# Feed-forward input of a 2048-frame encoder layer: gate and up products by turns instead of block by block

## The chip, the cores and the metric

The kernel runs on one core of a Trainium2 chip. The metric is the device time of one execution in microseconds (us). Engines are named as in the profile: PE (TensorE, the matmuls), PEld (TensorE's weight loads, beside PE), DVE (VectorE), ACT (ScalarE), POOL (GpSimd) and SP (SyncE, which issues all the large transfers of this stage in one queue).

## The reference, cut to what matters

```python
for l in range(DEPTH):                                   # DEPTH = 1, x: 2048 x 1024, fp32
    h = rmsnorm(x, mix_norm_g[l])
    proj = jnp.einsum('bsd,de->bse', h, w_in[l])
    q, k, v, u, vg = jnp.split(proj, split_pts, axis=-1)
    a = band_attention(q, k, v, q_norm_g[l], k_norm_g[l], rel_bias[l])
    g = spatial_gating(u, vg, sgu_norm_g[l], w_spatial[l], b_spatial[l])
    mix = jnp.concatenate([rmsnorm(a, att_out_norm_g[l]), rmsnorm(g, gmlp_out_norm_g[l])], axis=-1)
    x = x + jnp.einsum('bse,ed->bsd', mix, w_out[l])
    h = rmsnorm(x, ffn_norm_g[l])
    gate, up = jnp.split(jnp.einsum('bsd,df->bsf', h, w_ffn_in[l]), 2, axis=-1)
    x = x + jnp.einsum('bsf,fd->bsd', jax.nn.silu(gate) * up, w_ffn_out[l])
```

The change lies in the line with `gate, up` (1024 to 2 x 2816 columns) and in `silu(gate) * up`.

## The kernel before, in words

Every fp32 operand is split in two parts that PE takes at its faster rate: `split` (lines 86 to 88) writes the rounded value h with a cast on ACT (line 87) and the rest l with a subtraction on DVE (line 88); `mm3` (lines 90 to 93) makes a product of three matmuls: h by h (L91), h by l (L92), l by h (L93). So `wih` and `wil` are the two parts of a weight operand, and `yh` and `yl` those of an activation operand.

The stages follow each other: input projection, attention, output projection, feed-forward input (lines 701 to 797), feed-forward output. Both feed-forward matrices go by Winograd's scheme of seven products for a 2 x 2 block product.

**Activation operands.** For each of 16 row tiles, `operands(m)` transposes the normalized tile `h2` on PE (`pth`, L606), copies it to `hT` (ACT, L607), makes four sums t1 to t4 on POOL (L618 to L621) and writes seven operand pieces to memory in `y_d` (SP, L623). `prep(hf)` later loads the seven operands of one half of the rows (`ynat`, four transfers each, into the three buffers of the pool `gt`, which also hold the result tile `g`) and splits them into yh0..yh6 and yl0..yl6. There is one buffer for each of the seven, so those of the second half can be written only when the first half's last product with the same number is done.

**Weight operands.** `weights(p, s)` loads two raw tiles `wir` (512 KB each), makes four sums s1 to s4 on POOL (L733 to L736) and splits seven operands. s is 0 for gate and 1 for up, p is one of 11 pairs of column blocks. The operands stand in a ring of eight `wih` and eight `wil`.

**Products.** `block(w, ys, g, s)` runs the seven products of one side one after another, each of 4 x 3 matmuls of 128x512 into a PSUM bank. ACT copies v1 and v, DVE makes u2 and the sums `g` (gate) or `up`, ACT applies silu, POOL multiplies (L757). Two halves, 11 pairs, two sides, seven products and 12 matmuls are 3696 matmuls. After each pair, POOL and DVE make three sums `c` (L791 to L794), and SP writes `g` and `c` to `f_d` (L796, L797).

**Feed-forward output.** For each of 11 rounds the next stage loads an activation operand `ar` from `f_d` and a weight (`w11_0`, `w11_2`, ... in the first 11 rounds, in buffers of their own; later ones in `wor`), and splits them into ah, al, oh, ol.

**What sets the order.** The tile framework's scheduler sets each engine's order from the program's dependences and from when pool memory comes free; on PE the attention stage's order is written out by hand. A new pool takes the memory of closed ones, and its first writer then waits for their last reader. SP's transfers run through eight completion semaphores in turn, so an issue also waits until the transfer eight before it has landed.

Of the kernel before, what the change touches and what calls it, by code (L numbers as in the profile page):

```python
# [18 lines left out]
P = 128  # L19
# [12 lines left out]
NF = DFF // P  # L32
# [11 lines left out]
def block_kernel(ctx: ExitStack, tc: tile.TileContext, x, xT, w_in, mixg, qg, kg, bias, sgug, wsT, bsp, outg, w_out, ffng, w_fi, w_fo, out):  # L44
    nc = tc.nc
# [30 lines left out]
    def pool(stack, name, bufs, side="left", space=bass.MemoryType.SB):  # L76
        return stack.enter_context(tc.tile_pool(name=name, bufs=bufs, side=side if space != PSUM else None, space=space, reuse_waits="tile"))
# [8 lines left out]
    def split(hi, lo, src):  # L86
        nc.scalar.copy(hi, src)  # L87
        nc.vector.tensor_sub(lo, src, hi.bitcast(F32))  # L88

    def mm3(ps, lh, ll, rh, rl, first, last):  # L90
        nc.tensor.matmul(ps, lhsT=lh, rhs=rh, start=first, stop=False)  # L91
        nc.tensor.matmul(ps, lhsT=lh, rhs=rl, start=False, stop=False)  # L92
        nc.tensor.matmul(ps, lhsT=ll, rhs=rh, start=False, stop=last)  # L93
# [4 lines left out]
    apool = {}  # L98
    bt, vt, qd, kw, pvs, sums, xm, gn, an, mh, ml, heads = ({} for _ in range(12))

    def open_attention(stack):
        for n, bufs in (("pr", 3), ("pp", 2), ("an", 2), ("sa", 4), ("vt", 6), ("bt", 1), ("qd", 2), ("kw", 5)):
            apool[n] = pool(stack, n, bufs, "right")


    woh, wol, mx = {}, {}, {}
# [138 lines left out]
    with ExitStack() as st:  # L245
# [240 lines left out]
        w = [None] * 4  # L486
# [20 lines left out]
        wr = raw.tile([P, G, P], F32, tag="raw", name="wsr")  # L507
# [12 lines left out]
        for hf in range(2):  # L520
            for b, unit in enumerate(blocks):
                for tl in range(8):
                    t = hf * 8 + tl
# [26 lines left out]
                w = nw  # L550


    with ExitStack() as st:
        st_att = st.enter_context(ExitStack())
        open_attention(st_att)
        st_wr.close()
        hp = pool(st_out, "h2", 1)
# [85 lines left out]
        def feed(k, whole):  # L643
            while fill:
                kind, f = fill[0]
                if kind in ("piece", "bank"):
                    if k < 1 or kind == "bank" and not whole:
                        break
                    f()
                    k -= 1  # L650
                elif kind == "operands":
                    operands(f)
                elif kind == "g":
                    load_xm(f)
# [13 lines left out]
        with tc.manual_schedule(engines={mybir.EngineType.PE}):  # L668
            for m in range(NE):
                an[m] = None  # L670
            for _ in range(3):
                k = feed(KT, True)
            for i in range(len(LATE) + 2):
                if i < len(LATE):
                    m, h = LATE[i]
# [7 lines left out]
                k = feed(k + 1, False)  # L683
                if 1 <= i <= len(LATE):
                    flip(*LATE[i - 1], sp)
                k = feed(k + 1, True)
                if i >= 2:
                    m, h = LATE[i - 2]
# [10 lines left out]


    with ExitStack() as st:
        gt, wr, sp3, wi = (pool(st, n, b, "right") for n, b in (("gt3", 3), ("wr3", 2), ("sum3", 1), ("wi3", 8)))
        yp = [pool(st, f"y{i}", 1) for i in range(2)]
        tm = pool(st, "tm3", 2)
        yp += [pool(st, f"y{i}", 1, "left" if i < 5 else "right") for i in range(2, 7)]
        cb = pool(st, "cb3", 1, "right")
        pb = [pool(st, f"pb{i}", 4, space=PSUM) for i in range(2)]

        def bank(s):
            return pb[s].tile([P, 512], F32, tag="b", name="bank")  # L710

        def prep(hf):
            ys = []
            for o in range(7):
                yh = yp[o].tile([P, 4, 512], F32R, tag="yh", name=f"yh{hf}{o}")
                yl = yp[o].tile([P, 4, 512], F32R, tag="yl", name=f"yl{hf}{o}")
                ys.append((yh, yl))
                r = gt.tile([P, 4, 512], F32, tag="g", name="ynat")
                for i in range(4):
                    nc.sync.dma_start(r[:, :, i * P : (i + 1) * P], y_d[hf][o][i].rearrange("p (k t) -> p k t", k=4))  # L720
                for k in range(0, 4, 2):
                    split(yh[:, k : k + 2], yl[:, k : k + 2], r[:, k : k + 2])
            return ys

        def weights(p, s):
            r = []
            for i in range(2):
                t = wr.tile([P, 2, 512], F32, tag="wr", name="wir")
                nc.sync.dma_start(t, w_fi[2 * p + i, s])
                r.append(t)  # L730
            x11, x12, x21, x22 = r[0][:, 0], r[0][:, 1], r[1][:, 0], r[1][:, 1]
            s1, s2, s3, s4 = (sp3.tile([P, 512], F32, tag=f"s{i}", name=f"s{i}") for i in range(4))
            nc.gpsimd.tensor_add(s1, x21, x22)  # L733
            nc.gpsimd.tensor_sub(s2, s1, x11)  # L734
            nc.gpsimd.tensor_sub(s3, x11, x21)
            nc.gpsimd.tensor_sub(s4, x12, s2)  # L736
            ops = []
            for src in (x11, s2, s1, s3, x12, s4, x22):
                h = wi.tile([P, 4, P], F32R, tag="wih", name="wih")
                l = wi.tile([P, 4, P], F32R, tag="wil", name="wil")  # L740
                split(h, l, src.rearrange("p (k f) -> p k f", k=4))
                ops.append((h, l))
            return ops

        def product(bk, w, y):
            for k in range(4):
                mm3(bk, w[0][:, k], w[1][:, k], y[0][:, k], y[1][:, k], k == 0, k == 3)

        def block(w, ys, g, s):
            def emit(i, bk, add):  # L750
                if s == 0:
                    nc.vector.tensor_tensor(g[:, i], bk, add, op=ALU.add)
                    nc.scalar.activation(g[:, i], g[:, i], AF.Silu)
                else:
                    t = tm.tile([P, 512], F32, tag="up", name="up", bufs=1)
                    nc.vector.tensor_tensor(t, bk, add, op=ALU.add)  # L756
                    nc.gpsimd.tensor_tensor(g[:, i], t, g[:, i], op=ALU.mult)  # L757

            ba, bb, bc, bd = (bank(s) for _ in range(4))
            v1 = tm.tile([P, 512], F32, tag="v1", name="v1")  # L760
            u2 = tm.tile([P, 512], F32, tag="u2", name="u2")
            v = tm.tile([P, 512], F32, tag="v", name="v", bufs=1)
            product(ba, w[0], ys[0])
            nc.scalar.copy(v1, ba)
            product(bb, w[1], ys[1])
            nc.vector.tensor_tensor(u2, bb, v1, op=ALU.add)
            product(bc, w[2], ys[2])
            nc.scalar.copy(v, bc)
            nc.gpsimd.tensor_tensor(v, v, u2, op=ALU.add)
            product(bd, w[3], ys[3])  # L770
            nc.vector.tensor_tensor(u2, bd, u2, op=ALU.add)
            emit(3, bd, v)
            product(ba, w[4], ys[4])
            emit(0, ba, v1)
            product(bc, w[5], ys[5])
            emit(1, bc, v)
            product(bd, w[6], ys[6])
            emit(2, bd, u2)

        w = weights(0, 0)  # L780
        for hf in range(2):
            ys = prep(hf)
            for p in range(NF // 2):
                g = gt.tile([P, 4, 512], F32, tag="g", name="g")
                for s in range(2):
                    block(w, ys, g, s)
                    nx = 2 * p + s + 1
                    if nx < NF or hf == 0:
                        w = weights(*divmod(nx % NF, 2))
                c = cb.tile([P, 3, 512], F32, name="c", tag="c")  # L790
                nc.gpsimd.tensor_add(c[:, 0], g[:, 1], g[:, 3])  # L791
                nc.gpsimd.tensor_sub(c[:, 1], c[:, 0], g[:, 0])
                nc.gpsimd.tensor_sub(g[:, 1], g[:, 0], g[:, 1])
                nc.vector.tensor_sub(c[:, 2], g[:, 2], c[:, 1])  # L794
                hs = slice(hf * 512, (hf + 1) * 512)
                nc.sync.dma_start(f_d[p][0:4, :, hs].rearrange("o p t -> p o t"), g)  # L796
                nc.sync.dma_start(f_d[p][4:7, :, hs].rearrange("o p t -> p o t"), c)  # L797


    with ExitStack() as st:  # L800
        xo, t4, wk0, wt, ca, cb = (
            pool(st, n, b, "right") for n, b in (("xo4", 8), ("tm4", 4), ("wk40", 1), ("wt4", 3), ("ca4", 1), ("cb4", 1)))
        at, ar, wk, wr = (pool(st, n, b) for n, b in (("at4", 2), ("ar4", 3), ("wk4", 1), ("wr4", 4)))
        pb = [pool(st, f"pb4{i}", 4, space=PSUM) for i in range(2)]
# [118 lines left out]
```

## Time and profile before

| | us |
|---|---|
| median of 3 runs | 2212.45 (2211.03 to 2214.38) |
| the profiled execution, its own time | 2214.4 |
| span of that execution | 2212.6 |
| feed-forward input on PE | 919.4 to 1785.6 of the span |
| PE busy | 2162.9, 98% of the span |

PE is busy 98% of the span, so a gain can come only from stretches in which PE waits or runs at a lower clock. The profile's rows give start and duration in us of the span. In a timeline row "x2" joins neighbours of one kind, and the bracket at its end is the idle time of that engine just before it and what ended it. In a table by windows each engine has its busy time and, in brackets, the number of instructions; PEclk is the granted share of TensorE's full clock. Matmuls are pipelined: a duration of 0.39 us goes with a start every 0.226 us.

### The profile page before, as it was taken

How to read it: one execution, taken by the hardware profiler on the slowest of the kernel's cores; microseconds unless marked ns; L12 is line 12 of the kernel's file. 1: busy time of each engine (PE TensorE's matmuls, PEld its weight loads, DVE VectorE, ACT ScalarE, POOL GpSimd, SP SyncE). 2: the span in 40 equal slices, each digit the busy share in tenths (PEclk: the TensorE clock that was granted, in tenths of full speed). 3: DMA queues.
4: the chain of work that ended last, by engine and by line, in shares of the span. 5: the costliest groups of instructions: out<-in, count | busy, mean ns of one | idle time of the engine just before them, and what ended most of it. 6: DMA issues, size and time to landing. Idle time of an engine off the chain costs nothing.

```text
span 2212.6 us, 31917 instructions
## 1 busy us (share of the span) xinstructions
PE 2162.9 (98%) x12090; PEld 1796.8 (81%) x12090; DVE 1275.4 (58%) x1809; ACT 899.7 (41%) x1639; POOL 912.4 (41%) x792
## 2 busy tenths in 40 slices
PE   8999999999999999799999998999999999999999
PEld 7888887887888888688888886888888888888787
DVE  3467435774667666685555558556555534545555
ACT  6444534552565665443333335333232323222322
POOL 1264113330002200756666575575656512603444
PEclk9999999999999999999999999999999999999999
DMA  7243615648878874832323236232322363833463
GB/s 253 86 124 119 233 58 162 172 135 260 284 229 275 264 241 145 291 132 91 116 90 116 96 128 194 92 123 91 114 100 94 111 238 133 290 122 119 157 234 135
DMA packets 183802, 356.60 MB, mean 161 GB/s; under 512 B 15328, under 2 KB 68576, under 8 KB 182112
## 3 DMA queue, kind: packets, MB, share of 16 engines
q1 hardware_dynamic: 183504, 354.55, 48.5%
q8 instruction: 95, 1.56, 0.3%
q14 instruction: 59, 0.48, 0.1%
q10 hardware_dynamic: 144, 0.00, 0.0%
HBM read 253.83 MB, written 100.66 MB: 160 GB/s over the span
## 4 chain that ended last, share of the span: by engine, by line
PE 71%; issue 11%; POOL 6%; DVE 6%; DMA 3%; ACT 1%; SPq 1%; DVEq 0%; POOLq 0%; ACTq 0%
PE bank L91 16%; PE bank L93 16%; PE bank L92 16%; PE ps L91 5%; PE ps L92 5%; PE ps L93 5%; DVE wil L88 1%; PE S L177 1%; PE pt L204 1%; PE po L91 1%; PE po L93 1%; PE po L92 1%; POOL g L757 1%; PE pv L216 1%; POOL rhr L83 1%
## 5 line engine op out<-in xcount | busy, mean ns | idle before, releaser
L92 PE MATMUL bank<-yl,wih 128*128 128x512 f32 x1232 | 481.3, 391 | 5.8 <-DVE yl L88 5.8
L91 PE MATMUL bank<-yh,wih 128*128 128x512 f32 x1232 | 478.3, 391 | 8.6 <-ACT wih L87 3.8
L93 PE MATMUL bank<-yh,wil 128*128 128x512 f32 x1232 | 477.2, 390 | 0.0
L91 PEld LDWEIGHTS bank<-yh,wih 128*128 128x128 f32 x1232 | 232.2, 189 | 59.6 <-ACT wih L87 4.2
L92 PEld LDWEIGHTS bank<-yl,wih 128*128 128x128 f32 x1232 | 232.3, 189 | 57.0 <-DVE yl L88 8.8
L93 PEld LDWEIGHTS bank<-yh,wil 128*128 128x128 f32 x1232 | 232.1, 188 | 48.2
L91 PE MATMUL ps<-wh,xh 128*128 128x512 f32 x640 | 252.2, 399 | 8.1 <-ACT wh L87 8.1
L92 PE MATMUL ps<-wl,xh 128*128 128x512 f32 x640 | 251.4, 394 | 2.5 <-DVE wl L88 2.5
L93 PE MATMUL ps<-wh,xl 128*128 128x512 f32 x640 | 251.2, 393 | 0.0
L92 PE MATMUL bank<-ol,ah 128*128 128x512 f32 x616 | 240.0, 390 | 0.0
L91 PE MATMUL bank<-oh,ah 128*128 128x512 f32 x616 | 237.8, 390 | 1.3 <-ACT oh L87 1.3
L88 DVE TENSOR_TENSOR wil<-s,wih 128x512 fp32r<-128x512 f32 x176 | 178.4, 1051 | 89.3 <-ACT wih L87 89.1
L88 DVE TENSOR_TENSOR al<-ar,ah 128x1024 fp32r<-128x1024 f32 x77 | 110.2, 1431 | 203.7 <-ACT ah L87 203.7
L93 PE MATMUL bank<-oh,al 128*128 128x512 f32 x616 | 222.0, 391 | 2.1 <-DVE al L88 2.1
L87 ACT CAST ah<-ar 128x1024 fp32r<-128x1024 f32 x77 | 81.2, 1055 | 292.6 <-PE bank L92 275.4
L87 ACT CAST wih<-s 128x512 fp32r<-128x512 f32 x176 | 100.9, 617 | 177.5 <-POOL s L734 136.8
L757 POOL TENSOR_TENSOR g<-up,g 128x512 f32<-128x512 f32 x88 | 138.2, 1571 | 79.4 <-DVE up L756 79.4
L91 PEld LDWEIGHTS ps<-wh,xh 128*128 128x128 f32 x640 | 121.2, 190 | 31.5 <-ACT wh L87 8.1
L92 PEld LDWEIGHTS ps<-wl,xh 128*128 128x128 f32 x640 | 121.1, 189 | 26.7 <-DVE wl L88 3.5
L93 PEld LDWEIGHTS ps<-wh,xl 128*128 128x128 f32 x640 | 121.0, 189 | 25.1
L87 ACT CAST wih<-wir 128x512 fp32r<-128x512 f32 x132 | 81.6, 618 | 143.6 <-PE bank L92 125.1
L733 POOL TENSOR_TENSOR s<-wir 128x512 f32<-128x512 f32 x44 | 58.7, 1334 | 194.3 <-DMA wir<-in_w_fi 181.1
(182 smaller groups left out, 4089.8 us busy)
## 6 DMA issues: line engine op xcount, KB each, us to landing
wir<-in_w_fi SPq DMA_DIRECT2D x88, 512.0 KB, 3.3
ar<-f_d SPq DMA_DIRECT2D x77, 512.0 KB, 3.3
kTw<-kT_d SPq DMA_DIRECT2D x96, 320.0 KB, 4.0
f_d<-g SPq DMA_DIRECT2D x22, 1024.0 KB, 4.0
wr<-in_w_in SPq DMA_DIRECT2D x40, 512.0 KB, 5.1
f_d<-c SPq DMA_DIRECT2D x22, 768.0 KB, 4.2
wor<-in_w_fo SPq DMA_DIRECT2D x66, 256.0 KB, 3.4
ynat<-y_d SPq DMA_DIRECT2D x56, 256.0 KB, 4.7
```

Source lines behind the costliest of these rows:

```text
L83: nc.gpsimd.tensor_tensor(r, ms, nhalf[:, :k], op=ALU.pow)
L87: nc.scalar.copy(hi, src)
L88: nc.vector.tensor_sub(lo, src, hi.bitcast(F32))
L91: nc.tensor.matmul(ps, lhsT=lh, rhs=rh, start=first, stop=False)
L92: nc.tensor.matmul(ps, lhsT=lh, rhs=rl, start=False, stop=False)
L93: nc.tensor.matmul(ps, lhsT=ll, rhs=rh, start=False, stop=last)
L177: nc.tensor.matmul(S[:, i, :hw], lhsT=q[:, p], rhs=k[:, i * hw : (i + 1) * hw], start=p == 0, stop=p == 1)
L204: nc.tensor.transpose(pt[:, i], pr[:, i * P : (i + 1) * P], ident)
L216: nc.tensor.matmul(o, lhsT=a[:, i], rhs=vt[m + 1 - nk + i][:, c, h * HD : (h + 1) * HD], start=n == 0, stop=n == len(seq) - 1)
L733: nc.gpsimd.tensor_add(s1, x21, x22)
L757: nc.gpsimd.tensor_tensor(g[:, i], t, g[:, i], op=ALU.mult)
```

## The change

The products run in the order half, pair, product o, side s: a gate product and the up product with the same activation operand come in turn. `generate(n)` makes the weight operand for the n-th product and is called five products ahead of its use. A ring of six `wih`/`wil` takes the place of eight. Raw tiles have a buffer of their own for each side and row (four in all, as before), reloaded when their last reader is done (`w_raw`, called with o = 5 and o = 6 of the pair before). The sums are made in place: x21+x22 over x21, and s4 over s2. The temporaries `v1`, `u2`, `v` have one buffer for each side. The pools are opened in another order and on other sides, and a pad `skip2` of 64 floats is put into the attention's pool `sa`. The number of matmuls, casts, sums and transfers is the same.

```diff
@@ open_attention
             apool[n] = pool(stack, n, bufs, "right")
+            if n == "sa":
+                apool[n].tile([P, 64], F32, name="skip2", bufs=1)
@@ feed-forward input
-        gt, wr, sp3, wi = (pool(st, n, b, "right") for n, b in (("gt3", 3), ("wr3", 2), ("sum3", 1), ("wi3", 8)))
-        yp = [pool(st, f"y{i}", 1) for i in range(2)]
-        tm = pool(st, "tm3", 2)
-        yp += [pool(st, f"y{i}", 1, "left" if i < 5 else "right") for i in range(2, 7)]
+        yp = {0: pool(st, "y0", 1, "right")}
+        gt, wr, wi, sp3 = (pool(st, n, b, "right") for n, b in (("gt3", 3), ("wr3", 1), ("wi3", 6), ("sum3", 1)))
+        for i in (1, 2):
+            yp[i] = pool(st, f"y{i}", 1)
+        tm = pool(st, "tm3", 1)
+        for i in (3, 4, 5, 6):
+            yp[i] = pool(st, f"y{i}", 1, "left" if i < 5 else "right")
...
-        def weights(p, s):
...
+        def w_raw(p, s, i):
+            t = wr.tile([P, 2, 512], F32, tag=f"r{s}{i}", name="wir")
+            nc.sync.dma_start(t, w_fi[2 * p + i, s])
+            raws[p, s, i] = t
+
+        def w_sums(p, s):
+            x11, x21, x22 = raws[p, s, 0][:, 0], raws[p, s, 1][:, 0], raws[p, s, 1][:, 1]
+            s3 = sp3.tile([P, 512], F32, tag=f"s3{s}", name="s3")
+            s2 = sp3.tile([P, 512], F32, tag=f"s2{s}", name="s2")
+            raws[p, s, 2] = (s2, s3)
             nc.gpsimd.tensor_sub(s3, x11, x21)
+            nc.gpsimd.tensor_add(x21, x21, x22)
+            nc.gpsimd.tensor_sub(s2, x21, x11)
+
+        def w_op(p, o, s):
+            (x11, x12), (s1, x22), (s2, s3) = ((raws[p, s, i][:, 0], raws[p, s, i][:, 1]) if i < 2 else raws[p, s, i] for i in range(3))
+            if o == 5:
+                nc.gpsimd.tensor_sub(s2, x12, s2)
+            src = (x11, s2, s1, s3, x12, s2, x22)[o]
+            h = wi.tile([P, 4, P], F32R, tag="wih", name="wih")
+            l = wi.tile([P, 4, P], F32R, tag="wil", name="wil")
+            split(h, l, src.rearrange("p (k f) -> p k f", k=4))
+            ops.append((h, l))
+
+        order = [(hf, p, o, s) for hf in range(2) for p in range(NP) for o in range(7) for s in range(2)]
+
+        def generate(n):
+            if n >= len(order):
+                return
+            hf, p, o, s = order[n]
+            w_op(p, o, s)
+            if n + 14 < len(order):
+                q = (p + 1) % NP
+                if o == 5:
+                    w_raw(q, s, 0)
+                if o == 6:
+                    w_raw(q, s, 1)
+                    w_sums(q, s)
...
+        for s in range(2):
+            for i in range(2):
+                w_raw(0, s, i)
+            w_sums(0, s)
+        AHEAD = 5
+        for n in range(AHEAD):
+            generate(n)
+        for n, (hf, p, o, s) in enumerate(order):
+            if (p, o, s) == (0, 0, 0):
+                ys = prep(hf)
+            if (o, s) == (0, 0):
                 g = gt.tile([P, 4, 512], F32, tag="g", name="g")
...
+            generate(n + AHEAD)
+            if o < 4:
+                banks[s, o] = pb[s].tile([P, 512], F32, tag="b", name="bank")
+            bk = banks[s, (0, 1, 2, 3, 0, 2, 3)[o]]
+            product(bk, ops[n], ys[o])
+            use(o, s, bk, g)
```

How the built programs differ at four places (names carry the program's own buffer numbers).

PE where feed-forward input begins, before: the products with yh_11679, yh_11690 and yh_11701 (the first three) are ahead of `pth`, the transposes of the last row tile; here the end of the third.

```order
L91 MATMUL bank<-yh_11701,wih 128x512
L92 MATMUL bank<-yl_11702,wih 128x512
L93 MATMUL bank<-yh_11701,wil 128x512
L606 MATMUL pth<-ident,h_11545 128x128 x8
L91 MATMUL bank<-yh_11679,wih 128x512
```

The same place in the changed program, from the last matmul of the output projection (`po`) on:

```order
L93 MATMUL po<-woh_5184,ml_11364 128x512
L608 MATMUL pth<-ident,h_11546 128x128 x8
L91 MATMUL bank<-yh_11678,wih 128x512
L92 MATMUL bank<-yl_11679,wih 128x512
L91 MATMUL bank<-yh_11678,wih 128x512
```

The three products that stood ahead of the last transposes stand behind them.

POOL and its first weight sums, before: they (L733 to L736) stand among the sums of row tile 13 (t_11312 to t_11315), two tiles ahead of the last.

```order
L619 TENSOR_TENSOR t_11313<-hT,t_11312 128x512
L733 TENSOR_TENSOR s_11643<-wir 128x512
L735 TENSOR_TENSOR s_11645<-wir 128x512
L81 TENSOR_SCALAR rfm<-ssf 128x1
L621 TENSOR_TENSOR t_11315<-b_11309,t_11313 128x512
L734 TENSOR_TENSOR s_11644<-s_11643,wir 128x512
```

In the changed program (t_11565 to t_11568 are the last row tile's sums; L741 to L748 are weight sums):

```order
L83 TENSOR_TENSOR rfr<-rfm,nhalf 128x1
L622 TENSOR_TENSOR t_11567<-hT 128x512
L620 TENSOR_TENSOR t_11565<-hT,b_11562 128x512
L621 TENSOR_TENSOR t_11566<-hT,t_11565 128x512
L623 TENSOR_TENSOR t_11568<-b_11562,t_11566 128x512
L741 TENSOR_TENSOR s_11644<-wir 128x512
L741 TENSOR_TENSOR s_11653<-wir 128x512
```

The first weight sums moved behind the last row tile's. On ACT the first `wih` of the changed program stands behind yh of operand 4, and its buffer lies on memory of the last row tile's t_11568: it waits until SP's write of that tile to `y_d` (the last of the seven writes) has landed.

DVE where the second half of the rows begins, before (yl10 to yl16 are the second half's operands, wil weight operands):

```order
L88 TENSOR_TENSOR yl10_15057<-ynat_15058,yh10_15056 128x1024 x2
L766 TENSOR_TENSOR u2_14906<-bank_14902,v1_14905 128x512
L88 TENSOR_TENSOR yl11_15068<-ynat_15069,yh11_15067 128x1024 x2
L88 TENSOR_TENSOR wil_15026<-s1_15014,wih_15025 128x512
L88 TENSOR_TENSOR wil_15030<-s0_15013,wih_15029 128x512
L88 TENSOR_TENSOR wil_15034<-s2_15015,wih_15033 128x512
```

In the changed program:

```order
L88 TENSOR_TENSOR yl10_15012<-ynat_15013,yh10_15011 128x1024 x2
L88 TENSOR_TENSOR wil_14912<-wir_14817,wih_14911 128x512
L780 TENSOR_TENSOR up_14927<-bank_14739,v1_14752 128x512
L88 TENSOR_TENSOR wil_14931<-wir_14840,wih_14930 128x512
L88 TENSOR_TENSOR yl11_15023<-ynat_15024,yh11_15022 128x1024
L776 TENSOR_TENSOR g_14715<-bank_14796,v_14809 128x512
```

Before, yl10 comes when the last up block's first product has run; now it comes in the last pair's ninth product, and the others follow between the drains of both sides.

SP at the end of the stage, before (f_d_193 is written by the last pair; w_0, w_2, w_4 are the first weights of feed-forward output, ar its activations):

```order
L797 DMA f_d_192<-c 128x3x512
L811 DMA w_0_18476<-in_w_fo 128x512
L811 DMA w_2_18512<-in_w_fo 128x512
L841 DMA ar<-f_d_183 128x1024
L841 DMA ar<-f_d_184 128x1024
L841 DMA ar<-f_d_185 128x1024
L841 DMA ar<-f_d_186 128x1024
L841 DMA ar<-f_d_187 128x1024
L811 DMA wor<-in_w_fo 128x512 x4
L796 DMA f_d_193<-g 128x4x512
L811 DMA w_4_18548<-in_w_fo 128x512
```

In the changed program:

```order
L830 DMA f_d_193<-g 128x4x512
L845 DMA w_4_18461<-in_w_fo 128x512
L831 DMA f_d_193<-c 128x3x512
L845 DMA w_6_18497<-in_w_fo 128x512
L845 DMA w_8_18533<-in_w_fo 128x512
L845 DMA w_10_18569<-in_w_fo 128x512
L845 DMA w_12_18605<-in_w_fo 128x512
L845 DMA w_14_18641<-in_w_fo 128x512
L845 DMA w_16_18677<-in_w_fo 128x512
L845 DMA w_0_18389<-in_w_fo 128x512
L845 DMA w_2_18425<-in_w_fo 128x512
```

The loads of w_0 and w_2 moved from ahead of the last pair's write to nine and ten places behind it. PE's order changed with them: before, the first two rounds of feed-forward output stand among the last products of feed-forward input; now the first matmul of feed-forward output (with oh, the cast of w_0) stands behind the last product.

## Rows read from the trace of the kernel before

**Rows 1.** Windows: length, busy us (instructions) by engine, clock, DMA share, GB/s.

```profile
919.00:1000.00 81.00, 72.95 (x312) 58.20 (x311) 66.33 (x60) 36.86 (x57) 54.20 (x36) 0.98 0.53 180
...
1100.00:1200.00 100.00, 100.00 (x443) 82.81 (x442) 58.51 (x75) 34.28 (x59) 59.73 (x43) 1.00 0.28 96
...
1786.00:1900.00 114.00, 112.67 (x498) 92.97 (x497) 47.47 (x43) 36.67 (x50) 28.93 (x20) 1.00 0.52 183
```

**Rows 2.** PE's waits from 895 to 1800: total us, times, longest.

```profile
PE bank L92 <- DVE yl L88: 5.8, 7, 2.8
PE bank L91 <- ACT wih L87: 3.8, 1, 3.8
```

**Rows 3.** Timeline of PE from 914 to 952, where the stage begins.

```profile
919.42 0.39 PE L91 MATMUL bank<-yh,wih 128*128 128x512 f32 x1
922.57 0.50 PE L92 MATMUL bank<-yl,wih 128*128 128x512 f32 x1 [2.76 <-DVE yl L88]
...
937.13 1.17 PE L606 MATMUL pth<-ident,h 128*128 128x128 f32 x8 [2.87 <-DVE h L597]
```

**Rows 4.** Timelines of DVE, ACT and POOL around the same place.

```profile
918.93 1.38 DVE L589 TENSOR_TENSOR xm<-po,xm 128x512 f32<-128x512 f32 x2 [6.12 <-PE po L93]
...
921.29 1.06 ACT L594 ACTIVATE jk<-xm 128x1024 bf16<-128x1024 f32 x1
...
937.84 1.08 ACT L607 COPY hT<-pth 128x512 f32<-128x512 f32 x2 [1.96 <-issue]
...
923.74 2.15 POOL L621 TENSOR_TENSOR t<-b,t 128x512 f32<-128x512 f32 x1
...
943.28 2.17 POOL L621 TENSOR_TENSOR t<-b,t 128x512 f32<-128x512 f32 x1
```

**Rows 5.** Line 623 (writes to y_d), 900 to 955: from issue to landing.

```profile
DMA to landing us min/median/max: 2.0/4.8/7.7
```

**Rows 6.** Timeline of PE at the half boundary, behind the wait of 3.8 us.

```profile
1380.62 0.63 PE L92 MATMUL bank<-yl,wih 128*128 128x512 f32 x1
1381.05 0.63 PE L93 MATMUL bank<-yh,wil 128*128 128x512 f32 x1
...
1384.88 0.51 PE L93 MATMUL bank<-yh,wil 128*128 128x512 f32 x1
```

**Rows 7.** Windows: the half boundary and two steady pairs, 76 us each.

```profile
1318.00:1394.00 76.00, 68.86 (x287) 55.17 (x286) 56.72 (x57) 34.31 (x52) 45.11 (x28) 0.96 0.60 187
...
1200.00:1276.00 76.00, 76.00 (x337) 62.94 (x336) 40.78 (x54) 25.72 (x44) 48.16 (x34) 1.00 0.30 104
```

**Rows 8.** Tile yl from 1318 to 1394: durations ns min/median/max, first and last start.

```profile
L88 DVE TENSOR_TENSOR yl<-ynat,yh x14: 1206/1834/2319, 1337.5 to 1375.5; 128x1024 fp32r<-128x1024 f32 x14
```

**Rows 9.** Groups by line of DVE and of POOL in the steady pairs, 1200 to 1276.

```profile
L88 DVE TENSOR_TENSOR wil<-s,wih 128x512 fp32r<-128x512 f32 x16 | 14.7, 957 | 6.6 <-ACT wih L87 6.6
L88 DVE TENSOR_TENSOR wil<-wir,wih 128x512 fp32r<-128x512 f32 x12 | 8.2, 684 | 0.0
...
L736 POOL TENSOR_TENSOR s<-wir,s 128x512 f32<-128x512 f32 x4 | 5.2, 1296 | 0.3
```

**Rows 10.** Timelines at the stage's end: PE, POOL, SP, ACT; last, tile w's landings.

```profile
1785.23 0.39 PE L93 MATMUL bank<-yh,wil 128*128 128x512 f32 x1
...
1789.07 1.28 POOL L757 TENSOR_TENSOR g<-up,g 128x512 f32<-128x512 f32 x1
...
1764.25 0.82 SPq L811 DMA_DIRECT2D w<-in_w_fo  x2
...
1790.38 0.38 SPq L796 DMA_DIRECT2D f_d<-g  x1
...
1792.42 5.31 SPq L811 DMA_DIRECT2D w<-in_w_fo  x7
...
1795.57 0.62 ACT L87 CAST oh<-w 128x512 fp32r<-128x512 f32 x1 [2.51 <-DMA w<-in_w_fo]
...
DMA to landing us min/median/max: 2.6/5.2/6.3
```

More of the change, by code (lines that the diff above doesn't have):

```diff
@@ L701, in block_kernel @@
     with ExitStack() as st:
-        gt, wr, sp3, wi = (pool(st, n, b, "right") for n, b in (("gt3", 3), ("wr3", 2), ("sum3", 1), ("wi3", 8)))
-        yp = [pool(st, f"y{i}", 1) for i in range(2)]
-        tm = pool(st, "tm3", 2)
-        yp += [pool(st, f"y{i}", 1, "left" if i < 5 else "right") for i in range(2, 7)]
+        yp = {0: pool(st, "y0", 1, "right")}
[5 more added lines that the diff above has]
+            yp[i] = pool(st, f"y{i}", 1, "left" if i < 5 else "right")
         cb = pool(st, "cb3", 1, "right")
         pb = [pool(st, f"pb{i}", 4, space=PSUM) for i in range(2)]
-        def bank(s):
-            return pb[s].tile([P, 512], F32, tag="b", name="bank")
+        NP = NF // 2
         def prep(hf):
@@ L723, in prep @@
             return ys
-        def weights(p, s):
[L726 to L734, printed above, removed]
-            nc.gpsimd.tensor_sub(s3, x11, x21)
[L736 to L743, printed above, removed]
+        raws, ops = {}, []
@@ L747, in product @@
                 mm3(bk, w[0][:, k], w[1][:, k], y[0][:, k], y[1][:, k], k == 0, k == 3)
[L749 to L783, printed above, removed]
-                g = gt.tile([P, 4, 512], F32, tag="g", name="g")
[L785 to L789, printed above, removed]
+        def emit(g, s, i, bk, add):
+            if s == 0:
+                nc.vector.tensor_tensor(g[:, i], bk, add, op=ALU.add)
+                nc.scalar.activation(g[:, i], g[:, i], AF.Silu)
+            else:
+                t = tm.tile([P, 512], F32, tag="up", name="up")
+                nc.vector.tensor_tensor(t, bk, add, op=ALU.add)
+                nc.gpsimd.tensor_tensor(g[:, i], t, g[:, i], op=ALU.mult)
@@ new lines, in block_kernel, with use, temp @@
+        banks, temps = {}, {}
+        def use(o, s, bk, g):
+            def temp(n):
+                temps[s, n] = tm.tile([P, 512], F32, tag=f"{n}{s}", name=n)
+                return temps[s, n]
+            if o == 0:
+                nc.scalar.copy(temp("v1"), bk)
+            elif o == 1:
+                nc.vector.tensor_tensor(temp("u2"), bk, temps[s, "v1"], op=ALU.add)
+            elif o == 2:
+                v, u2 = temp("v"), temps[s, "u2"]
+                nc.scalar.copy(v, bk)
+                nc.gpsimd.tensor_tensor(v, v, u2, op=ALU.add)
+            elif o == 3:
+                u2 = temps[s, "u2"]
+                nc.vector.tensor_tensor(u2, bk, u2, op=ALU.add)
+                emit(g, s, 3, bk, temps[s, "v"])
+            else:
+                emit(g, s, o - 4, bk, temps[s, ("v1", "v", "u2")[o - 4]])
@@ new lines, in block_kernel @@
+        for s in range(2):
[9 more added lines that the diff above has]
+            if (o, s) == (0, 0):
+                g = gt.tile([P, 4, 512], F32, tag="g", name="g")
+            generate(n + AHEAD)
[4 more added lines that the diff above has]
+            use(o, s, bk, g)
+            if (o, s) == (6, 1):
```

## The prediction

> **What bounds the kernel now.** I read first the table by windows [rows 1]. From 1100 to 1200 PE is busy for all of 100.00 us and starts 443 matmuls of this stage: 0.2257 us each, 2.71 us for a product of 12. So most of the stage has nothing to give, and what a different order is worth is decided in three places: where the stage begins, at the change from the first to the second half of the rows, and where it ends. The reader should see in the waits [rows 2] that in nearly 900 us PE's largest sums are 5.8 us for yl and 3.8 us for one wih.
>
> *Begin.* The window from 919 to 1000 has 312 PE instructions [rows 1]; without 8 transposes and one matmul of the projection they are 303 of this stage, worth 68.4 us of 80.6: 12 us are lost. The timeline [rows 3] shows how: the first product starts at 919.42, waits 2.76 us for yl, and the last row tile's transposes (pth) come only at 937.13, again behind a wait. Products run in between, so PE starves but isn't idle.
>
> *Half boundary.* In the 76 us around it PE is busy 68.86 [rows 7], 7.1 idle. Behind the wait of 3.8 us about 13 matmuls start 0.43 us apart instead of 0.2257 (half clock) [rows 6], 2.7 us more: 10 us lost.
>
> *End.* From 1786 to 1900 498 matmuls, worth 112.4, take 114: 1.6 us lost [rows 1]. It is small because the weights w_0 and w_2 were issued at 1764.25, 21 us before the last product ended [rows 10].
>
> **The change part by part.** Nothing is removed: 308 casts of weights (44 sides of seven), 176 weight sums and 88 raw loads stay. What counts is where they stand.
>
> *Steady pairs: 0.* Here DVE is busy 40.8 and POOL 48.2 of 76 us [rows 7], in either order the same work. Each operand is made five products (13.5 us) ahead. A raw tile is reloaded when its operands are split, about 7 products ahead of use, and load, sums and cast fit in that. PE is already full, so a shorter wait for a temporary brings nothing: 0, between -1 and +1.
>
> *Half boundary: -8.* Before, the second half's seven yh and yl had to be written between the last up block and the next blocks, block by block. Fourteen yl of 1.83 us [rows 8] are 25.7 us. Now each y has 12 products, 32 us, between its last use and the next, and the seven are spread over two pairs. DVE's load there is the steady 40.8 plus 25.7: 66.5 of 76 us [rows 7, 8]. I lined up DVE's new row order with those durations, wil at 0.68 to 0.96 [rows 9]: from yl10, behind the ninth product of the last pair, to yl16, each yl comes 2 to 9 us before its product, and one wil of the next pair's fifth gate operand comes 2 us late. So 2 us of the 10 remain: -8. Bounds: all 10 gone, or 6 remaining because ACT stands in order behind ynat loads: -10 to -4.
>
> What two engines do to each other there speaks against some of it. A weight sum on POOL takes 1.30 us; a wil from raw data takes 0.68 us, one from a sum 0.96 in the mean [rows 9], and yl goes from 1.21 to 2.32 [rows 8]. The Trainium skill, "SBUF — State Buffer", section "SBUF: two separate sides", says that a DVE instruction with two SBUF inputs and a GpSimd instruction share a port pair under an exclusive lock, so that one blocks for the whole of the other. By that rule the short durations would have to be laid end to end: 14 yl at 1.21, 28 wil at 0.68, 34 POOL instructions at 1.30 make 80 us in 76, about 4 us too much, and the gain would be 4 instead of 8. It changes only where in my bounds the value lies, and the steady windows with PE at 100% show the same lock doing no harm.
>
> *Begin: +14.* The three products that stood ahead of pth stand behind it, and the first wih waits for the last row tile's final write to y_d. The path, from rows of before: xm is complete at 920.3 to 921.2 and its squares at 922.4 [rows 4]. POOL is free at 925.9, when the tile ahead is done [rows 4], and since four weight sums no longer stand between, the two scalar steps and h2 on DVE end at about 929 (before, h2 ended near 937). Transposes 1.2 and copies 2.0: hT at 931.5. Before, hT ended at 938.9 and the last of the four sums on POOL at 945.45 [rows 4], 6.5 us later; at 1.3 to 2.17 each they take 5.2 to 8.7: the last ends at 937 to 940. SP then issues seven writes, which stand among ynat loads in the same queue; the last goes out at 938 to 940. Landing: 2.0 to 7.7, median 4.8 [rows 5]; I take 4.3, since the other loads are mostly done. One cast, 0.62, and PE starts at 943.5 (941 to 946). Behind wih on ACT are queued the casts yh5, yh6 and the copies of v1; behind them on PE every product. Lost: 943.5 - 919.65 = 23.9, plus about 2 at half clock after such a pause [rows 6], against 12 now; 23.9 + 2 - 12 = +14. The first sums come only then too, but two products (raw x11) need none. Bounds: 941 and no wait for the next wil, +10; 946 and 3 us for a wil behind four yl, +19.
>
> *End: +15.* Call S the start of the last product's last matmul (1785.23 before). Now nothing of feed-forward output is mixed in, and its first matmul needs w_0, issued nine places behind f_d<-g of the last pair. That write waits for DVE's last up (0.7), POOL's last multiplication (1.28): S + 2.5. Before, it went out at 1790.38 and the transfer nine places behind it at 1797.3 (the last of the seven in that row) [rows 10], landing 5.2 later: 12.1 from the write. So w_0 lands at S + 14.6, its cast takes 0.62, and PE, which would have gone on at S + 0.2, starts at S + 15.2. Add 2 at half clock, take away the 1.6 lost now: 15.0 + 2 - 1.6 = +15. Lower bound: the queue's spacing is shorter since fewer loads precede, w_0 issued 5.2 after the write (when the transfer eight earlier lands) and landed in the shortest 2.6: +10. Upper: the write only at S + 5.15, as before: +19. Before, 48 matmuls of two rounds, 10.8 us, covered just this chain; that cover is gone.
>
> **Sum.** On the profiled execution: 2214.4 + 0 - 8 + 14 + 15 = 2235.4. That execution lies 1.95 above the median 2212.45, so on the median 2233.5. With all bounds on one side: 2212.45 - 1 - 10 + 10 + 10 = 2221 and 2212.45 + 1 - 4 + 19 + 19 = 2247.
>
> **Rivals.** *One gap is nearly closed.* If the first wih isn't held by the write but only by yh4 ahead of it on ACT (ynat of operand 4 landing near 932.5, two casts, then wih), PE starts at about 937 and the begin costs +7; if at the end the weights come as early as the lower bound, +10. Time with one or both: 2222 to 2227. For it: before, raw weights and casts were ready 18 us ahead, so no engine is short of time. Against: the order puts the cast behind the write.
>
> *The other side: both gaps hidden.* The place is the first weight at either end. If the first wih is cast before 922.57 (when before had its first yl) and w_0 lands before the last product ends, nothing is lost there, even the 5 us of waits for yl at the start partly go, and the boundary's 8 remain: 2212.45 - 8 - 0 to 6 = 2198 to 2204. It decides at whether pth and w_0 stand ahead in the order. Against it are the built order and SP's one queue, in which w_0 can't pass f_d<-g.
>
> *A new wait in every pair.* If a raw load, its sums and casts took over 13.5 us more than planned, PE would wait in each of 22 pairs; 1 us each gives 2212.45 + 21 + 22 = 2256. Against: POOL and DVE have 28 and 35 us free in 76 [rows 7].
>
> *It cancels.* Boundary 10 gained, both ends cheap by an early landing: within 0.2%.
>
> **How the numbers follow.** 0.2% is 4.4 us, about what a measurement of this kernel can tell from no change. Forecast as summed, 2221 to 2247: 0.66. One gap nearly closed, 0.16 (slower by over 0.2% too). A new wait in every pair, 0.06. Both gaps hidden, 0.07, faster. Cancels, 0.05. So faster 0.07, same 0.05, slower 0.88. The time is the forecast's, 2234. The range goes from 2216, below the first rival's times, to 2250, past the forecast's upper bound.
>
> **What would show it.** Begin: PE idle from 919.7 to about 943 but for pth, ended by ACT wih, and that wih behind the landing of the last y_d write. Boundary: no wait above 2 us, no half clock. End: PE idle some 15 us, ended by ACT oh, and this by w_0 landing some 12 us after f_d<-g. Between: 443 matmuls in 100 us. It is wrong if PE's first product starts before 935, if w_0 is on the chip before the last product ends, or if windows between the three places fall below 99.

## The result, and the profile after

The changed kernel takes 2237.11 us (2233.88 to 2238.22, 4 runs) against 2211.74 (2210.05 to 2214.38) for the kernel before on the same chip: ratio 1.0111, 95% interval 1.0094 to 1.0129. It is 1.1% slower, inside the range and 3 us above the 2234 that was forecast. The profiled execution took 2236.06, its span is 2234.3, 21.7 us more than before. One of the four executions of the version with four raw tiles below took 5567.49 us, and its time there is that of the other three.

One sentence ahead of the prediction is wrong: the kernel before had two raw weight tiles, not four (`wr3` had 2 buffers, and a block loads two). The change doubles them, and the experiments show that this matters.

The windows of the changed kernel (length, busy us and instructions by engine, clock, DMA share, GB/s) answer [rows 1] and the first row of [rows 7]:

```profile
919.00:1000.00 81.00, 58.52 (x238) 47.43 (x239) 53.42 (x51) 30.96 (x48) 47.83 (x33) 0.81 0.40 133
1100.00:1200.00 100.00, 100.00 (x443) 82.81 (x442) 60.12 (x73) 34.38 (x60) 60.20 (x43) 1.00 0.31 112
1318.00:1394.00 76.00, 74.20 (x325) 60.43 (x324) 60.12 (x57) 32.79 (x49) 50.65 (x31) 1.00 0.55 176
1420.00:1780.00 360.00, 360.00 (x1590) 298.07 (x1589) 220.64 (x263) 123.87 (x213) 233.35 (x161) 1.00 0.33 116
1786.00:1900.00 114.00, 98.57 (x429) 81.19 (x428) 37.16 (x39) 31.74 (x44) 18.37 (x13) 0.94 0.40 138
```

In the first window 238 instructions stand where 312 stood, in the last 429 where 498 stood, and at the half boundary PE is now busy 74.2 of 76 us instead of 68.9. Between these places PE is full, as before. PE's waits from 895 to 1900 (total us, times, longest), against [rows 2], which end at 1800:

```profile
PE bank L91 <- ACT wih L87: 17.2, 2, 15.6
PE bank L91 <- ACT oh L87: 15.4, 1, 15.4
PE pth L608 <- DVE h L599: 7.6, 1, 7.6
PE bank L93 <- DVE wil L88: 4.1, 4, 2.1
```

The waits for yl are gone; two long waits for a first weight have come, one at each end of the stage.

To see where time is won or lost, I put the start of each of PE's 5544 matmuls into `bank` beside that of the same number before. The differences, in us, positive when later than before:

| place (time before) | changed kernel | what it says |
|---|---|---|
| projection's last matmul (919.2) | -3.4 | attention's end got faster |
| 1035 | +14.9 | the begin costs 18.3 from there |
| 1341 | +14.9 | steady pairs cost nothing |
| 1490 | +7.7 | half boundary -7.2 |
| 1762 | +7.7 | steady again |
| 1832 | +23.2 | end +15.5 |
| last matmuls | +21.7 | feed-forward output -1.5 |

The begin, PE, POOL, ACT and SP of the changed kernel, against [rows 3, 4]:

```profile
923.78 1.94 PE L608 MATMUL pth<-ident,h 128*128 128x128 f32 x8 [7.57 <-DVE h L599]
...
941.35 0.80 PE L91 MATMUL bank<-yh,wih 128*128 128x512 f32 x1 [15.63 <-ACT wih L87]
...
952.15 0.50 PE L93 MATMUL bank<-yh,wil 128*128 128x512 f32 x1 [2.06 <-DVE wil L88]
...
931.78 2.12 POOL L623 TENSOR_TENSOR t<-b,t 128x512 f32<-128x512 f32 x1
...
940.02 1.26 POOL L741 TENSOR_TENSOR s<-wir 128x512 f32<-128x512 f32 x1 [1.56 <-DMA y_d<-t]
...
940.68 1.14 ACT L87 CAST wih<-wir 128x512 fp32r<-128x512 f32 x2 [8.69 <-DMA y_d<-t]
...
934.51 1.10 SPq L625 DMA_DIRECT2D y_d<-t  x2
```

PE starts its first product when ACT has cast wih, ACT waits 8.69 us for the write of t to `y_d`, and that write went out at about 935. The bracket of the cast names the releaser: it is memory that is waited for, not the raw weights, which were there.

The end, PE, SP and ACT, against [rows 10]:

```profile
1791.31 0.39 PE L93 MATMUL bank<-yh,wil 128*128 128x512 f32 x1
...
1807.12 3.56 PE L91 MATMUL bank<-oh,ah 128*128 128x512 f32 x8 [15.43 <-ACT oh L87]
...
1761.10 0.38 SPq L830 DMA_DIRECT2D f_d<-g  x1
...
1793.93 0.37 SPq L830 DMA_DIRECT2D f_d<-g  x1
1794.35 0.50 SPq L845 DMA_DIRECT2D w<-in_w_fo  x1
1794.94 0.99 SPq L831 DMA_DIRECT2D f_d<-c  x1
1795.98 7.27 SPq L845 DMA_DIRECT2D w<-in_w_fo  x10
...
1806.45 1.76 ACT L87 CAST oh<-w 128x512 fp32r<-128x512 f32 x3 [16.08 <-DMA w<-in_w_fo]
```

The first of these writes of g is that of the pair before the last. The last pair's goes out 2.6 us after the last matmul's start, w_0 follows among the ten, and ACT sits 16 us until it has landed.

### The profile page after: what moved, and what is told of

It is laid out like the page before. It is cut to its first block, busy times and chain, and to the rows that moved or that the text cites. A ratio compares the mean times of both kernels' runs of the same rounds, so it can differ in the third digit from the quotient of the medians.

```text
span 2234.3 us, 32028 instructions
## 1 busy us (share of the span) xinstructions
PE 2160.9 (97%) x12090; PEld 1797.2 (80%) x12090; DVE 1295.2 (58%) x1809; ACT 901.9 (40%) x1639; POOL 920.1 (41%) x792
## 4 chain that ended last, share of the span: by engine, by line
PE 53%; DMA 2%; DVE 2%; SPq 1%; issue 1%; POOL 1%; ACT 0%; DVEq 0%; ACTq 0%; POOLq 0%
PE bank L91 18%; PE bank L93 18%; PE bank L92 18%; DMA ynat<-y_d 1%; DVE yl L88 1%; SPq L723 0%; DMA y_d<-t 0%; DVE wil L88 0%; DMA w<-in_w_fo 0%; SPq L845 0%; DMA b<-y_d 0%; POOL t L621 0%; DVE xo L894 0%; POOL wir L742 0%; DMA wir<-in_w_fi 0%
## 5 line engine op out<-in xcount | busy, mean ns | idle before, releaser
L91 PE MATMUL bank<-oh,ah 128*128 128x512 f32 x616 | 239.9, 392 | 15.4 <-ACT oh L87 15.4
L88 DVE TENSOR_TENSOR wil<-s,wih 128x512 fp32r<-128x512 f32 x132 | 134.0, 1017 | 122.6 <-ACT wih L87 122.6
L87 ACT CAST wih<-s 128x512 fp32r<-128x512 f32 x132 | 81.9, 622 | 303.6 <-POOL s L743 158.3
L88 DVE TENSOR_TENSOR wil<-wir,wih 128x512 fp32r<-128x512 f32 x176 | 195.4, 1111 | 6.3 <-ACT wih L87 6.3
L87 ACT CAST wih<-wir 128x512 fp32r<-128x512 f32 x176 | 108.9, 621 | 188.3 <-PE bank L92 178.0
L781 POOL TENSOR_TENSOR g<-up,g 128x512 f32<-128x512 f32 x88 | 122.8, 1395 | 108.9 <-DVE up L780 80.6
L91 PEld LDWEIGHTS bank<-oh,ah 128*128 128x128 f32 x616 | 116.6, 190 | 40.3 <-ACT oh L87 15.8
```

## The experiments

The built programs say why both first weights are late. A pool's tiles lie at fixed places: in the changed kernel the first wih lies on 143.5 to 145.5 KB of each partition, where attention's last t lay (142.5 to 144.5), and w_0 on 195.5 to 197.5, inside a buffer of g (191.5 to 199.5). Before, the first operands lay on 151.5 and up, w_0 on a raw tile. The two places are not alike. The t tile is itself read by the last write to `y_d`. The buffer of g under w_0 is that of the pair before the last, whose write went out at 1761.10; the last pair's g lies on 199.5 to 207.5. So no reader of these bytes held w_0 that long: SP's built order did, in which w_0 stands behind the last write. Which rule of the scheduler puts it there no run tells. My theory was that the layout, which the new pool order brought, costs both gaps, and the turns bring the boundary's gain; the rival was that turns cause the gaps. Differences by place below are those of the table above, each against the profile of the kernel before. That kernel was timed again beside the versions, with medians of 2214.12, 2214.23 and 2210.98, so the medians of different versions can be compared to within some 3 us.

**Only the end's layout.**

```diff
-        xo, t4, wk0, wt, ca, cb = (
-            pool(st, n, b, "right") for n, b in (("xo4", 8), ("tm4", 4), ("wk40", 1), ("wt4", 3), ("ca4", 1), ("cb4", 1)))
+        wk0, xo, t4, wt, ca, cb = (
+            pool(st, n, b, "right") for n, b in (("wk40", 1), ("xo4", 8), ("tm4", 4), ("wt4", 3), ("ca4", 1), ("cb4", 1)))
```

> The changed kernel with one edit: in feed-forward output the pool of w_0 and w_2 (wk40) is opened first on its side, so that these two tiles lie on yl0, free some 30 us before the stage ends, and no longer on a buffer of g, which is read by the last write to f_d. Theory (the end gap is the late load of w_0 behind that write): both loads go out ahead of f_d<-g, PE's gap of 15.4 us at the end falls below 2 us, and the time falls by 14 to 16 us, from 2237 to 2221 to 2223. Rival (the gap comes from gate and up by turns, since nothing of the next stage is mixed in): the gap stays above 10 us, 2232 to 2237. Begin and half boundary as in the changed kernel by either.

Measured 2222.93, 14 us less. SP loads w_0 some 30 us ahead of the last write, and PE's timeline has only this wait at the end, with some eight matmuls at half clock behind it:

```profile
1757.56 0.50 SPq L845 DMA_DIRECT2D w<-in_w_fo  x1
...
1791.31 0.50 PE L92 MATMUL bank<-ol,ah 128*128 128x512 f32 x1 [1.79 <-DVE ol L88]
```

The end costs +2.1 instead of +15.5, although still nothing of the next stage is mixed in. Begin and boundary stay (+12.0 at 1035, then -8.3).

**Only the begin's layout.**

```diff
-        yp = {0: pool(st, "y0", 1, "right")}
-        gt, wr, wi, sp3 = (pool(st, n, b, "right") for n, b in (("gt3", 3), ("wr3", 1), ("wi3", 6), ("sum3", 1)))
-        for i in (1, 2):
-            yp[i] = pool(st, f"y{i}", 1)
+        wr, gt, wi, sp3 = (pool(st, n, b, "right") for n, b in (("wr3", 1), ("gt3", 3), ("wi3", 6), ("sum3", 1)))
+        yp = {i: pool(st, f"y{i}", 1) for i in range(2)}
         tm = pool(st, "tm3", 1)
-        for i in (3, 4, 5, 6):
+        for i in (2, 3, 4, 5, 6):
```

> The changed kernel with another layout of the pools: y0 on the left as in the kernel before, and the raw weights ahead of gt on the right, so that weight operands and sums lie on attention buffers that are free early, while w_0 and w_2 still lie on a buffer of g. Theory (the begin's gap is the first wih's buffer on the last row tile's t): the first sums and casts are made before the projection ends, PE's first product starts right behind the projection instead of at 941, and 14 to 17 us go, less up to 3.4 us that come back if weight work stands among the last attention tiles again: 2220 to 2226; the end gap stays at 15. Rival (the begin is late because both sides' first operands and sums must be made): the first product starts after 930 all the same, 2232 to 2237.

Measured 2220.10. At 1035 it stands at -2.4 instead of +14.9; the end keeps +15.5. The rival is out for the begin as well.

**Both.** As above with `gt` ahead of `wr`, as in the kernel before; ring and sums stand in the changed kernel's order.

> The changed kernel with the layout of the kernel before (gt, raw weights, operands, sums on the right, y0 and y1 on the left): neither the first weight operand lies on the last row tile's t nor w_0 on g. Theory: both gaps go and the half boundary's gain of 7 us stays: 2237 - 15 - 15 = 2207, between 2203 and 2210, faster than the kernel before (2211.7). Rival (gate and up by turns causes the gaps): above 2225.

Measured 2199.47 (2199.05 to 2200.07), ratio to the kernel before 0.9932, 0.9915 to 0.9949. Gate and up by turns with the old layout is faster than both kernels, and below the 2203 to 2210 expected, since the begin gains too: -5.9 at 1035, then -7.4 at the boundary and -1.6 at the end. PE's waits in it from 1000 to 1800 are all that is left of the boundary:

```profile
PE bank L93 <- DVE wil L88: 2.1, 3, 1.0
PE bank L91 <- ACT wih L87: 1.5, 1, 1.5
```

**The new layout in the old kernel.**

```diff
+        y0 = pool(st, "y0", 1, "right")
         gt, wr, sp3, wi = (pool(st, n, b, "right") for n, b in (("gt3", 3), ("wr3", 2), ("sum3", 1), ("wi3", 8)))
-        yp = [pool(st, f"y{i}", 1) for i in range(2)]
+        yp = [y0, pool(st, "y1", 1)]
```

> The kernel before with one edit: the pool y0 is opened first and on the right, as in the changed kernel, so that its weight operands (a ring of eight) come to lie on the last row tile's t0 to t3 and w_0 on a buffer of g. Order of products, ring and sums stay block by block. Theory (layout makes both gaps): PE idles 10 to 22 us at the begin and 13 to 16 us at the end, half boundary unchanged: 2212 + 10 to 16 + 14 to 16 = 2236 to 2244. Rival (turns make the gaps): 2210 to 2214.

Measured 2242.20: block by block, with that one pool moved, the kernel before gets both gaps.

```profile
PE bank L91 <- ACT oh L87: 19.2, 1, 19.2
PE bank L91 <- ACT wih L87: 17.0, 2, 13.2
PE pth L606 <- DVE h L597: 7.6, 1, 7.6
```

So the layout is shown to be the cause of both gaps, by taking it away and by adding it (here the last pair's own g lies under w_0, on 191.5 to 199.5). The begin costs 11.1 here (-4.4 at the projection's end, +6.7 at 1035), the changed kernel's 18.3.

**The other 7 us of the begin.** In the old kernel with y0 on the right only operands lie on the t tiles; in the changed kernel the sums do too.

```diff
-        gt, wr, wi, sp3 = (pool(st, n, b, "right") for n, b in (("gt3", 3), ("wr3", 1), ("wi3", 6), ("sum3", 1)))
+        gt, wr, sp3, wi = (pool(st, n, b, "right") for n, b in (("gt3", 3), ("wr3", 1), ("sum3", 1), ("wi3", 6)))
```

> The changed kernel with the sums' pool opened ahead of the ring, so that only the weight operands lie on the last row tile's t0 to t3, as in the kernel before with y0 on the right, where the begin cost 11 us against 18 in the changed kernel. Theory (the 7 us between them are the sums' memory: products from the third on waited for sums made only after the writes): PE's first product starts at 937 to 941 and the later waits for wil and the second half-clock stretch go: 4 to 7 us less than 2237, 2230 to 2233. Rival (they come from gate and up needing twice the operands early): 2235 to 2238.

Measured 2230.87, 6.2 less, and +7.4 at 1035 instead of +14.9. The first product starts at 938.48 and the wait of 2.06 us for wil behind it is gone. The sums' memory was the other part.

**Turns undone, the rest kept** (on the version with both layouts repaired).

```diff
-        order = [(hf, p, o, s) for hf in range(2) for p in range(NP) for o in range(7) for s in range(2)]
+        order = [(hf, p, o, s) for hf in range(2) for p in range(NP) for s in range(2) for o in range(7)]
```

> The version with the old layout (2199.5) with one edit: the seven products of the gate side, then the seven of the up side, as before; ring of six, five ahead, four raw tiles and sums in place stay. Theory (the half boundary's gain is the turns': 12 instead of 6 products between an operand's last use and its next): the loss of some 10 us at the boundary comes back, +7 to +9, 2206 to 2209, and PE waits there for yl and wih again. At the begin a third of the early products' operands are needed sooner, 0 to +3. Rival (the gain comes from ring, raw tiles of their own or sums in place): within 2 us of 2199.5.

Measured 2205.48, 6.0 more. By place: boundary -4.2 instead of -7.4, and 2.0 at the begin. Only 3 of the 7 us at the boundary are the turns'; my theory said all of them, so it was wrong by more than half.

**Raw tiles.** What else could keep 4 us? The kernel before with room for the raw tiles of two blocks, paid for by a smaller ring (first added line), and the smaller ring alone as a control (second):

```diff
-        gt, wr, sp3, wi = (pool(st, n, b, "right") for n, b in (("gt3", 3), ("wr3", 2), ("sum3", 1), ("wi3", 8)))
+        gt, wr, sp3, wi = (pool(st, n, b, "right") for n, b in (("gt3", 3), ("wr3", 4), ("sum3", 1), ("wi3", 6)))
+        gt, wr, sp3, wi = (pool(st, n, b, "right") for n, b in (("gt3", 3), ("wr3", 2), ("sum3", 1), ("wi3", 6)))
```

> The kernel before with two sizes changed: four raw weight tiles instead of two, and a ring of six operands instead of eight to make room; products still block by block. Block by block on the changed kernel's structure had kept 4 of the 7 us gained at the half boundary. Theory (those 4 us are the raw tiles': with two, the sums of the next block stand behind the DVE work that frees them, one wih comes 3.8 us late and PE then runs at half clock): that wait and its half clock go, the waits for yl stay, 4 us less: 2208 to 2211. Rival (they come from operands made one by one, product by product): the wait of 3 to 4 us for wih stays, 2212 to 2216.

> The kernel before with a ring of six operands instead of eight and nothing else, so that the run with four raw tiles can be read. Theory (steady blocks have operands to spare): 443 matmuls in 100 us stay, boundary the same or 1 to 4 us worse: 2212 to 2217. Rival (a block's seven operands must stand together): every block waits, above 2225.

Four raw tiles: 2199.95 (2199.07 to 2202.77, three executions), ratio 0.9944 (0.9924 to 0.9964), better than expected. The boundary gains 4.2, the begin 6.1 at 1035, the end 1.0. The two kernels' waits from 1300 to 1450, before first:

```profile
PE bank L91 <- ACT wih L87: 3.8, 1, 3.8
PE bank L91 <- ACT v L768: 2.6, 2, 1.9
PE bank L91 <- DVE g L752: 1.0, 1, 1.0
PE bank L92 <- DVE yl L88: 0.8, 2, 0.5
```

```profile
PE bank L92 <- DVE yl L88: 6.2, 3, 4.5
```

The wait for wih and the half clock behind it are gone; a wait for yl is left, with eight matmuls at half clock behind it (1.6 us), and these the turns remove. Without any turns this version has most of what both repairs together bring: 6.1, 4.2 and 1.0 against 5.9, 7.4 and 1.6 by place, and the intervals of the two ratios overlap. The ring of six with two raw tiles takes 2230.92, as the rival said: PE waits 16 times for g, 10.2 us in all, and its lag grows from 4.9 us at 1035 to 10.2 at 1341. With four raw tiles the same ring holds the full rate. So a ring that is too small with one block's raw tiles is large enough with two.

**How far ahead.** On the version with both layouts repaired, three products ahead in a ring of four (shown), and four in a ring of five:

```diff
-        gt, wr, wi, sp3 = (pool(st, n, b, "right") for n, b in (("gt3", 3), ("wr3", 1), ("wi3", 6), ("sum3", 1)))
+        gt, wr, wi, sp3 = (pool(st, n, b, "right") for n, b in (("gt3", 3), ("wr3", 1), ("wi3", 4), ("sum3", 1)))
...
-        AHEAD = 5
+        AHEAD = 3
```

> The version with the old layout with weight operands made three products ahead in a ring of four instead of five in a ring of six. Theory (in steady pairs five ahead is more than needed, and only the half boundary, where DVE lags, draws on it): steady windows stay at 442 or 443 matmuls in 100 us, the boundary loses 2 to 5 us more, 2201 to 2206. Rival (depth counts everywhere): 0.5 to 1 us in each of 22 pairs, 2210 to 2222.

> The version with the old layout with four products ahead in a ring of five. Three ahead cost 14 us, all at the half boundary, where POOL ran its instructions one behind another at 2.25 us each and one sum came 11 us late. Theory (POOL's lag at the boundary is what the depth covers, 2.7 us for each product): 4 to 8 us slower than five ahead, 2203 to 2208, by a wait for wih at the boundary of 3 to 6 us; steady windows full. Rival (threshold: three is too few for the ring as such, four is enough): 2199 to 2201.

Three ahead: 2213.72, 14 us more where 2 to 5 were said, though with the steady windows full (1325 matmuls from 1000 to 1300, as with five). The boundary alone is 10 us worse (+2.6 instead of -7.4), and it is one place, in the timelines of POOL, ACT and PE:

```profile
1358.95 2.25 POOL L825 TENSOR_TENSOR g<-g 128x512 f32<-128x512 f32 x1
1361.17 2.24 POOL L746 TENSOR_TENSOR s<-wir,s 128x512 f32<-128x512 f32 x1
1363.37 2.24 POOL L779 TENSOR_TENSOR g<-up,g 128x512 f32<-128x512 f32 x1
1365.57 1.26 POOL L740 TENSOR_TENSOR wir<-wir 128x512 f32<-128x512 f32 x1
1366.90 1.60 POOL L741 TENSOR_TENSOR s<-wir 128x512 f32<-128x512 f32 x1
...
1368.54 0.62 ACT L87 CAST wih<-s 128x512 fp32r<-128x512 f32 x1
...
1369.21 0.79 PE L91 MATMUL bank<-yh,wih 128*128 128x512 f32 x1 [10.95 <-ACT wih L87]
```

POOL runs one instruction behind another, many at 2.25 us instead of 1.28 while DVE makes the yl, and the sum that PE needs is last in that row. Four ahead: 2197.72 (ratio 0.9937, 0.9922 to 0.9952), no slower than five (0.9932, 0.9915 to 0.9949). So there is a step between three and four, not 2.7 us for each product as I expected; depth and ring were changed together, so which of the two makes it is not shown.

**The 3.4 us ahead of the stage.** In the kernel before a first wil of 1.51 us stands on DVE ahead of a residual addition at 890; PE waits and then runs ten matmuls at half clock. Two more orders of the four pools on the right move the first operands to memory that is free later (one added line each):

```diff
-        gt, wr, wi, sp3 = (pool(st, n, b, "right") for n, b in (("gt3", 3), ("wr3", 1), ("wi3", 6), ("sum3", 1)))
+        wi, wr, gt, sp3 = (pool(st, n, b, "right") for n, b in (("wi3", 6), ("wr3", 1), ("gt3", 3), ("sum3", 1)))
+        wr, wi, gt, sp3 = (pool(st, n, b, "right") for n, b in (("wr3", 1), ("wi3", 6), ("gt3", 3), ("sum3", 1)))
```

> The version with the old layout, with the ring of weight operands first on the right, then raw tiles, result tiles, sums. The first operands come to lie on attention buffers that are free some 20 us later, so that no weight subtraction stands on DVE ahead of the residual additions of row tiles 13 and the first half of 14. Theory (the kernel before and the old layout lose 3.4 us at 890 because the first wil, 1.51 us, stands ahead of such an addition, PE waits 2.15 us and falls to half clock for some 10 matmuls): that goes, 2196, between 2194 and 2198, projection ended at 915.8 instead of 919.3. Rival (the 3.4 us go with the weight work's amount, not its place): 2199 to 2201.

> The same aim with raw tiles first, then the ring, result tiles, sums: the first wil of all stands one residual addition later still, and w_0 is loaded just ahead of the last write to f_d instead of eight places. Theory: the 3.4 us at 890 go as well, but two operands fewer are ready when the stage begins, +0 to +4, and w_0, issued within 2 us of f_d<-g, may come late at the end: at its usual landing of 5 us PE waits 0 to 5 us. 2195 to 2205. Rival (place of w_0 within the queue counts for nothing once ahead of the write): equal to the sister version within 2 us.

First: 2198.66 (2196.24 to 2200.49), not told from 2199.47. The wait at 890 did fall, but a wait of 4.44 us for h2 at 916 took its place: the weight work now meets the tile after. Second: 2207.89 (ratio 0.9975, 0.9961 to 0.9989), above the 2195 to 2205 expected, with a wait of 3.5 us for a residual addition at the stage's begin and 1.2 for oh at its end. In these two orders, moving this work about within attention's end shifts the loss and doesn't remove it.

## Why the prediction was right, and where it was not

**Steady pairs, 0: right.** 1590 matmuls from 1420 to 1780, PE busy all 360 us. One thing in a steady pair was not foreseen: a wait of 1.6 us for wih one pair behind the boundary. DVE's work was not the same either: 43.85 us instead of 40.78 from 1200 to 1276, with a wil from a raw tile at 999 ns in the mean instead of 684. It cost nothing, for PE stayed full.

**Begin, +14: right in cause, 14.9 at 1035, but of two errors that nearly cancel, which is luck.** The whole path ran earlier than I had it: hT was ready at 926.4 instead of 931.5, the last sum at 933.9 instead of 937 to 940, the first product at 941.35 instead of 943.5; the last write's landing, sized at 4.3 us, took 5.4 and gave part of that back. The projection itself ended 3.4 us sooner, which I had not counted, since no wil stood in front of a residual addition. Against that, after the pause PE ran some 20 matmuls at half clock in two stretches (4 us, not 2), and waited 2.06 for a wil. From the projection's end the begin cost 18.3.

**Half boundary, -8: right in size (-7.2), wrong in more than half of the cause.** I put all of it down to the products between an operand's last use and its next, and left out that the raw tiles were doubled. The runs give 3 us to the turns and 4 to the raw tiles. The late wil that I found by lining up DVE's rows was there, as two waits:

```profile
1381.86 0.50 PE L93 MATMUL bank<-yh,wil 128*128 128x512 f32 x1 [0.74 <-DVE wil L88]
...
1385.82 0.50 PE L93 MATMUL bank<-yh,wil 128*128 128x512 f32 x1 [0.91 <-DVE wil L88]
```

The rule of the page "SBUF — State Buffer" in the Trainium skill, section "SBUF: two separate sides", would have left 4 us lost. Its mechanism agrees with POOL's 2.25 us beside yl against 1.28 alone; laid end to end over two pairs it said too much, for 1.7 us of waits were measured there.

**End, +15: right, 15.5.** f_d<-g at 2.6 us after the last matmul's start (2.5 said), the cast of w_0 at 15.1 (14.6 said), PE's pause 15.4 (15.0 said), half clock 1.6 (2 said).

**Rivals.** Neither gap was nearly closed, none hidden, and no wait in every pair came. Between the two profiled executions the difference is 21.7 us, where the sum said 21; terms that I had left out (the late wil and more half clock at the begin, -3.4 and -1.5 elsewhere) nearly cancel. That the sum came so close is therefore partly luck. The 3 us between forecast and measured median are scatter of the two medians: the profiled execution of before lay 2.6 above its median, that of the changed kernel 1.1 below.

## What to carry to other kernels

When a change reorders pools, look up what each first tile of a stage comes to lie on: an operand whose raw weight is on the chip in time is still late if its own buffer's last reader is a store of the stage before (the begin), and a load can come to stand behind such a store in its queue (the end). Here two such places cost more than the change's idea could bring. Take the order of the pools and the order of the work apart in an experiment before judging either: the idea that lost 1.1% gains 0.7% with the old layout, and more raw buffers alone, without the idea, bring 0.6%. For depth ahead, look at the one place where a helper engine lags, not at the steady rate.

## What was not expected of the hardware

The clock doesn't answer to a pause of some 2 us in the same way each time. Behind a wait of 2.15 us for the same residual addition PE fell to half clock in the kernel before, and behind 2.14 us it did not in the version with both layouts repaired (granted clock from 892 to 897: 0.66 and 1.00):

```profile
892.23 0.50 PE L91 MATMUL po<-woh,mh 128*128 128x512 f32 x1 [2.15 <-DVE xm L589]
...
893.81 0.63 PE L91 MATMUL po<-woh,mh 128*128 128x512 f32 x1
```

```profile
892.62 0.50 PE L91 MATMUL po<-woh,mh 128*128 128x512 f32 x1 [2.14 <-DVE xm L591]
...
893.67 0.40 PE L92 MATMUL po<-wol,mh 128*128 128x512 f32 x1
```

In feed-forward output the same happened near 2095: one wait of 2.1 us for al in both kernels (near 2115 in the changed one), and a granted clock of 0.83 in that stretch of 10 us before, 1.00 after. That is the 1.5 us of the table's last row. What decides it no run here tells.
